# The second feed-forward product: six of its seven block products again split into seven products of halves

## The chip, the cores and the metric

The kernel runs on one core of a Trainium2 chip. Such a core has a matrix engine (TensorE, PE in the profile, with its weight loads listed apart as PEld), three engines for elementwise work (VectorE = DVE, ScalarE = ACT, GpSimd = POOL), and a queue engine (SyncE = SP) that issues the transfers between the chip's memory (HBM, "DRAM" in the code), and the on-chip memory (SBUF). Matrix products are summed in PSUM. The metric is the time of one execution in microseconds of device time (us). Lower is better.

## The reference

One layer of an encoder on a sequence of 2048 tokens, width 1024, float32: a stick-breaking attention, and behind it a feed-forward part of width 2816, each between two normalisations with a gate. This case is about the feed-forward part, and there about its last product:

```python
def swiglu_ffn(h, w_in, w_out):
    g, u = jnp.split(h @ w_in, 2, axis=-1)
    return (jax.nn.silu(g) * u) @ w_out
...
x = x + gt_f * rms_norm(y, norm_g[i, 3])
```

The first product is 2048 x 1024 times 1024 x 5632, the second (its left operand is `silu(g) * u`, "the activations" below) 2048 x 2816 times 2816 x 1024.

## The kernel before, in words

**Three products for one.** Each float32 operand is split into a high part (a copy rounded to the matrix engine's float32r, by ACT) and a low part (the operand minus the high part, by DVE or GpSimd). `mm3` (L146) then gives three matmuls, high x high (L148), high x low (L149) and low x high (L150), into the same PSUM bank. Every operand that meets the matrix engine so costs one copy and one subtraction of its size. The kernel's clock is the *slice*: one `mm3`. After each slice `tick()` (L805) runs what `after(slices, ...)` (L799) has put off until then, and moves on every generator in the list `beside` by one step. The instructions of PE, ACT, DVE and GpSimd stand in the order in which this code emits them; the transfers on SP are put in order by a scheduler of the framework. Every engine works through its own list strictly in order, and SP too: a transfer that has to wait for an engine's result or for a free buffer holds up all transfers behind it.

**The first product** (lines s in the profile) takes the tokens as two pairs of 512 (s = 0, 1) and the hidden width as 22 chunks f of 128. For each of the 44 groups (s, f) a 2 x 2 block product is made of seven block products in place of eight (Strassen-Winograd), each of four slices: 28 slices a group. For the next group, DVE makes four sums of the weights (`left_add`, L1196), and ACT and DVE split seven blocks (`left_split`, L1213, L1214). What leaves PSUM is kept by ACT (`keep`, L1296: products 1, 5 and 6, in tiles p) or added by DVE (L1348 to L1364). GpSimd multiplies gate and up of one half (tile `one`, L1360), and four more of its additions per two groups (`act_sum`, L1314) make the block sums that the second product needs; all blocks are stored to DRAM (`put_act`, L1300). Products 5 and 6 are kept in tiles of the tag "w", of which there are three: the copy of product 6 of a group needs the buffer that the `one` of the group before sets free, and product 7, two products later, is accumulated in the bank that this copy reads.

**The second product** (lines o) is one more such block product: tokens in pairs of 512, the 22 chunks of the hidden width as 11 pairs (even and odd chunk, `GO` = 11), the 1024 columns as two halves. `OUT_PRODUCTS = [1, 2, 5, 6, 4, 7, 3]` are made one after another, each in eight steps (s, i) of 11 slices: 128 tokens, 512 columns. For a step, `a_load` and `a_split` (L1238 to L1245) bring and split the left operand, ACT and GpSimd; the right operand of a product, 11 tiles of 512 columns, is loaded (`b_load`), summed by DVE (`chain_make`, L1275) and split by ACT and DVE (`b_split`, L1281, L1282) while the product before it runs. `take` (L1449, L1455) adds the bank to one or two of the four running blocks (`totals`). The last two products end output rows: square sums, norm, gate, residual (`end_square` to `end_store`), and the store.

Of the kernel before, what the change touches and what calls it, by code (L numbers as in the profile page):

```python
# [16 lines left out]
P = 128  # L17
# [10 lines left out]
EPS = 1e-6  # L28
QK_SCALE = HD ** -0.5
# [53 lines left out]
def hybrid_trunk_kernel(  # L83
# [47 lines left out]
    act_s = {  # L131
        (product, s): dram.tile([P, 4, FC // 2, P], F32, name=f"act_s{product}_{s}")
        for product in range(1, 8) for s in range(NB // 2)
    }
# [1041 lines left out]
    groups = [(s, f if s == 0 else FC - 1 - f) for s in range(NB // 2) for f in range(FC)]  # L1176
# [46 lines left out]
    GO = FC // 2  # L1223
    OUT_PRODUCTS = [1, 2, 5, 6, 4, 7, 3]
    out_steps = [(at, s, i) for at in range(7) for s in range(NB // 2) for i in range(4)]
    NSTEP = len(out_steps) // 7
    GQ = 8

    left_out, right_out, chain, out_raw, totals, totals_at = {}, {}, {}, {}, {}, {}

    def a_load(m):
        at, s, i = out_steps[m]
        src = act_s[OUT_PRODUCTS[at], s][:, i]
        parts = [
            att.tile([P, 2, n, P], F32R, name=f"ol{m}_{t}", tag=t, bufs=BUFS[t])
            for t, n in (("qt", GQ), ("aT", GO - GQ))
        ]
        nc.sync.dma_start(f32(parts[0][:, 1]), src[:, :GQ])  # L1238
        nc.sync.dma_start(f32(parts[1][:, 1]), src[:, GQ:])
        left_out[m] = parts  # L1240

    def a_split(m):
        for hl in left_out[m]:
            nc.scalar.copy(hl[:, 0], f32(hl[:, 1]))
            nc.gpsimd.tensor_tensor(hl[:, 1], f32(hl[:, 1]), f32(hl[:, 0]), op=ALU.subtract)  # L1245
# [5 lines left out]
    def b_load(at, g, which):  # L1251
        par, half = block(which)
        raw = att.tile([P, BT], F32, name=f"br{at}_{g}", tag="a", bufs=BUFS["a"])
        nc.sync.dma_start(raw, wout[half, g, :, par])
        out_raw[at, g] = raw

    def chain_tile(version, g):

        if g < 8 and g % 2 == 0:
            tag = ("wraw", "qkn")[g // 2 % 2]  # L1260
            t = att.tile([P, 2, BT], F32, name=f"ch{version}_{g}", tag=tag, bufs=BUFS[tag])
            chain[g], chain[g + 1] = t[:, 0], t[:, 1]
        elif g >= 8:
            chain[g] = att.tile([P, BT], F32, name=f"ch{version}_{g}", tag="tmp", bufs=BUFS["tmp"])

    def chain_load(version, g, which):
        chain_tile(version, g)
        par, half = block(which)
        nc.sync.dma_start(chain[g], wout[half, g, :, par])

    def chain_make(at, g):

        raw = out_raw.pop((at, g))
        a, b = (raw, chain[g]) if OUT_PRODUCTS[at] in (6, 4) else (chain[g], raw)
        nc.vector.tensor_tensor(chain[g], a, b, op=ALU.subtract)  # L1275

    def b_split(at, g):
        src = out_raw.pop((at, g)) if OUT_PRODUCTS[at] in (1, 2) else chain[g]
        tag = "kt" if (at * GO + g) % 14 < 7 else "v"
        hl = att.tile([P, 2, BT], F32R, name=f"b{at}_{g}", tag=tag, bufs=BUFS[tag])  # L1280
        nc.scalar.copy(hl[:, 0], src)  # L1281
        nc.vector.tensor_tensor(hl[:, 1], src, f32(hl[:, 0]), op=ALU.subtract)  # L1282
        right_out[at, g] = hl
# [15 lines left out]
    def put_act(product, s, f, src):  # L1299
        nc.sync.dma_start(act_s[product, s][:, :, f // 2], src.rearrange("p (i t) -> p i t", i=4))  # L1300
# [85 lines left out]
    B_FIRST = {3: 0, 4: 1, 5: 2, 7: 7, 8: 8, 9: 9, 12: 3, 14: 4, 16: 5, 18: 6, 20: 10}  # L1386
    for n, (s, f) in enumerate(groups):
# [3 lines left out]
        for at, product in enumerate(PRODUCTS):  # L1391
            acc = banks_of[{1: 0, 6: 0, 7: 0, 4: 0, 5: 1, 3: 1, 2: 2}[product]]
            for k in range(H4):
# [19 lines left out]
                if s == 0 and 4 <= f < 4 + 2 * H4:  # L1413
                    kt, second = divmod(f - 4, 2)
                    if t == 5 and not second:
                        sums_load(1, kt)
                    if t in (15, 19):
                        sums_make(1, kt, 2 * second + (t == 19))
                    if t == 25 and second:
                        sums_store(1, kt)  # L1420

                if n in (FC - 1, FC):
                    at_next = t + 4 * len(PRODUCTS) * (n - FC + 1)
                    for m in range(14):
                        if at_next == 3 + 12 * m // 5:
                            right_load(1, m)
                        if at_next == 9 + 12 * m // 5:
                            right_split(1, m)
                if n + 1 == len(groups):
                    if t in B_FIRST:  # L1430
                        b_load(0, B_FIRST[t], "ec")
                    if t - 5 in B_FIRST:
                        b_split(0, B_FIRST[t - 5])
                    if t in (9, 13, 15):
                        a_load((9, 13, 15).index(t))
                    if t in (20, 24):
                        a_split((20, 24).index(t))
            after(1, taken, n, product, banks_of)

    x1_half, end_ssq, end_rstd = {}, {}, {}  # L1440

    def take(m, acc):

        at, s, i = out_steps[m]
        product = OUT_PRODUCTS[at]
        if product == 1:
            tag = "ht" if 4 * s + i < 5 else "whl"
            totals[s, i] = att.tile([P, 4, BT], F32, name=f"tot{s}_{i}", tag=tag, bufs=BUFS[tag])
            nc.scalar.copy(totals[s, i][:, 0], acc)  # L1449
            return  # L1450
        t = totals[s, i]
        for to, add in {
            2: [(1, 0)], 5: [(2, 0)], 6: [(0, 0), (2, 2)], 4: [(0, 0)], 7: [(0, 0), (3, 2)], 3: [(2, 2)],
        }[product]:
            nc.vector.tensor_tensor(t[:, to], acc, t[:, add], op=ALU.add)  # L1455
# [4 lines left out]
    def end_square(s, i, j, half):  # L1460
        junk = att.tile([P, BT], F32, name=f"ej{s}_{i}_{j}_{half}", tag="a", bufs=BUFS["a"])
        ssq = att.tile([P, 1], F32, name=f"es{s}_{i}_{j}_{half}", tag="rms_ssq", bufs=10)
        src = totals[s, i][:, ROW[j][half]]
# [14 lines left out]
    def end_store(s, i, j):  # L1478
        rstd = end_rstd.pop((s, i, j))
        r0 = (2 * s + j) * BT + i * P  # L1480
        for half, sl in enumerate(HALVES):
            t = x1_half.pop((s, i, j, half))
            y = totals[s, i][:, ROW[j][half]]
            nc.vector.scalar_tensor_tensor(t, y, rstd, t, op0=ALU.mult, op1=ALU.add)
            nc.sync.dma_start(out[r0 : r0 + P, sl], t)

    OUT_RAW = {1: "ec", 2: "oc"}
    SUM_OF = {5: ("ed", "ec"), 6: (None, "od"), 4: (None, "oc"), 7: ("od", "ed"), 3: ("od", None)}  # L1490

    def b_events(at):

        nxt = at + 1
        if nxt == 7:
            return
        product = OUT_PRODUCTS[nxt]
        if product in OUT_RAW:
            for g in range(GO):
                if g < 3:  # L1500
                    yield 5, 2 * g, (b_load, nxt, g, OUT_RAW[product])
                else:
                    yield 6, g - 2, (b_load, nxt, g, OUT_RAW[product])
        else:
            base, other = SUM_OF[product]
            for g in range(GO):
                step, at_slice = 2 + g // 3, 3 * (g % 3) + 1
                if base:
                    yield step, at_slice, (chain_load, nxt, g, base)
                if other:  # L1510
                    yield step, at_slice, (b_load, nxt, g, other)
                    yield step + 1, at_slice, (chain_make, nxt, g)
        for g in range(GO):
            if g < 3:
                yield 6, 3 * g + 1, (b_split, nxt, g)
# [76 lines left out]
```

## Time and profile before

| | us |
|---|---|
| median of 3 runs | 2873.65 (2872.4 to 2874.76) |
| the profiled execution | 2873.52 |
| its span on the core | 2871.1 |
| first feed-forward product, 1580 to 2442 us | 862 |
| second feed-forward product, 2442 to 2861 us | 419 |
| end behind the last matmul | some 10 |
| granted TensorE clock | 0.999 of full |

The profile is one execution, taken by the hardware profiler. A line such as "L148 PE MATMUL s<-r,l 128*128 128x512 f32 x1232 | 484.5, 393 | 7.0" is a group of instructions: source line, engine, operation, output<-inputs by the names of the tiles, the shape, how often; then the time in which at least one of them ran, the mean of one in ns, and the idle time of the engine just before them with what ended it. A matmul's record is its whole passage through the array, in which the next one has already begun: two in a row overlap, so a matmul's record is longer than the distance from one start to the next. A line of the waits reads: who waited, for whom, us in total, how often, the longest. A row of the stretches has the length of the stretch and then each engine's busy time and number of instructions, the clock, the mean busy share of the 16 DMA engines, and GB/s.

### The profile page before, as it was taken

What the parts mean: (1) busy time and instruction counts of PE and PEld (TensorE: products, weight loads), DVE (VectorE), ACT (ScalarE), POOL (GpSimd) and SP (SyncE); (2) the same over time, 40 slices, a digit from 0 to 9 for tenths busy, and PEclk for the clock granted to TensorE, in tenths of its full rate; (3) what the DMA queues carried; (4) which work ended last, traced back from release to release, by engine and by line L of the source; (5) the groups of instructions that cost most, each with busy time, mean ns of one, the idle gap of its engine ahead of it and who ended that gap; (6) DMA issues with size and microseconds to landing.
All of it is one profiled execution on the core that took longest, in us unless ns stands there. A gap on an engine that the chain in (4) does not pass through costs nothing.

```text
span 2871.1 us, 41790 instructions
## 1 busy us (share of the span) xinstructions
PE 2818.2 (98%) x13848; PEld 2335.4 (81%) x13848; DVE 2027.7 (71%) x2821; ACT 1634.5 (57%) x3265; POOL 1280.4 (45%) x2032
## 2 busy tenths in 40 slices
PE   7999999999999999999999999999999999999998
PEld 6788888888888888887888788888778888888887
DVE  6788888888888888888866666555776655134377
ACT  5787777787777877778645533334433333322243
POOL 1465666576576655666410122221222222544454
PEclk9999999999999999999999999999999999999999
DMA  8765546656665635546389544334453335545575
GB/s 324 270 210 165 187 156 223 209 174 227 191 210 184 216 113 175 191 133 227 97 292 313 193 136 151 121 92 163 130 165 118 111 93 175 190 132 153 181 226 186
DMA packets 239367, 516.84 MB, mean 180 GB/s; under 512 B 22320, under 2 KB 110384, under 8 KB 221488
## 3 DMA queue, kind: packets, MB, share of 16 engines
q1 hardware_dynamic: 239152, 514.18, 55.2%
q8 instruction: 109, 1.79, 0.3%
q14 instruction: 106, 0.87, 0.1%
HBM read 346.85 MB, written 118.49 MB: 162 GB/s over the span
## 4 chain that ended last, share of the span: by engine, by line
PE 88%; DVE 5%; DMA 3%; ACT 2%; issue 1%; POOL 0%; SPq 0%; DVEq 0%; POOLq 0%; ACTq 0%
PE s L148 9%; PE s L149 9%; PE s L150 9%; PE o L586 8%; PE z L507 8%; PE t L558 8%; PE pj L148 6%; PE pj L149 6%; PE pj L150 6%; PE o L149 5%; PE o L148 5%; PE o L150 4%; PE y L148 1%; PE y L150 1%; PE y L149 1%
## 5 line engine op out<-in xcount | busy, mean ns | idle before, releaser
L548 POOL TENSOR_TENSOR a<-a,w 128x512 f32<-128x512 f32 (+3 forms) x640 | 620.5, 969 | 221.7 <-DVE w L541 131.7
L541 DVE TENSOR_TENSOR_SCAN w<-z,c,begin 128x512 f32<-128x512 f32 x384 | 489.8, 1279 | 87.1 <-ACT z L526 68.3
L148 PE MATMUL s<-r,l 128*128 128x512 f32 x1232 | 484.5, 393 | 7.0 <-DVE p L1352 4.5
L149 PE MATMUL s<-r,l 128*128 128x512 f32 x1232 | 482.0, 391 | 0.0
L150 PE MATMUL s<-r,l 128*128 128x512 f32 x1232 | 481.8, 391 | 0.0
L524 ACT ACTIVATE a<-z 128x512 f32<-128x512 f32 (+3 forms) x640 | 347.5, 543 | 171.8 <-PE z L507 140.8
L586 PE MATMUL o<-aT,v 128*128 128x512 f32 (+3 forms) x1280 | 387.5, 384 | 0.1
L574 DVE TENSOR_TENSOR aT<-t,aT 128x512 fp32r<-128x512 f32 (+3 forms) x640 | 359.4, 595 | 23.7 <-ACT aT L568 23.2
L507 PE MATMUL z<-kt,qt 128*128 128x512 f32 (+3 forms) x1280 | 363.5, 365 | 0.0
L568 ACT CAST aT<-t 128x512 fp32r<-128x512 f32 (+3 forms) x640 | 314.2, 534 | 75.7 <-PE t L558 65.5
L526 ACT ACTIVATE z<-z 128x512 f32<-128x512 f32 (+3 forms) x640 | 345.1, 539 | 0.0
L1360 POOL TENSOR_TENSOR one<-p,p 128x512 f32<-128x512 f32 x44 | 71.1, 1616 | 595.3 <-issue 307.6
L148 PE MATMUL pj<-ht,w 128*128 128x512 f32 x768 | 312.7, 407 | 7.6 <-ACT ht L693 2.6
L149 PE MATMUL pj<-ht,w 128*128 128x512 f32 x768 | 305.3, 398 | 1.2 <-DVE ht L698 0.7
L558 PEld LDWEIGHTS t<-begin,a 128*128 128x128 f32 x2176 | 255.7, 141 | 58.5 <-DVE aT L574 10.3
L150 PE MATMUL pj<-ht,w 128*128 128x512 f32 x768 | 302.8, 394 | 0.0
L558 PE MATMUL t<-begin,a 128*128 128x128 f32 x2176 | 294.7, 273 | 7.9 <-DVE aT L574 6.8
L148 PEld LDWEIGHTS s<-r,l 128*128 128x128 f32 x1232 | 231.5, 188 | 60.2 <-DVE p L1352 6.3
L150 PEld LDWEIGHTS s<-r,l 128*128 128x128 f32 x1232 | 231.5, 188 | 50.8
L149 PEld LDWEIGHTS s<-r,l 128*128 128x128 f32 x1232 | 231.6, 188 | 50.2 <-issue 0.5
L507 PEld LDWEIGHTS z<-kt,qt 128*128 128x128 f32 x1280 | 230.5, 188 | 40.1
L536 DVE TENSOR_TENSOR_SCAN w<-z,begin 128x128 f32<-128x128 f32 (+3 forms) x256 | 208.7, 818 | 76.4 <-ACT z L526 66.6
(159 smaller groups left out, 4868.1 us busy)
## 6 DMA issues: line engine op xcount, KB each, us to landing
ht<-h_s SPq DMA_DIRECT2D x108, 1024.0 KB, 8.2
wi<-in_win SPq DMA_DIRECT2D x86, 512.0 KB, 4.1
qt<-qn SPq DMA_DIRECT2D x124, 256.0 KB, 4.7
ol_qt<-act_s SPq DMA_DIRECT2D x56, 512.0 KB, 3.7
act_s<-S SPq DMA_DIRECT2D x66, 256.0 KB, 4.2
br<-in_wout SPq DMA_DIRECT2D x66, 256.0 KB, 3.5
h_s<-ht SPq DMA_DIRECT2D x16, 1024.0 KB, 7.8
o_s<-os SPq DMA_DIRECT2D x128, 128.0 KB, 2.4
```

Of the source, the lines that this page charges most:

```text
L148: nc.tensor.matmul(acc, lhs[0], rhs[0], start=first, stop=False, **kw)
L149: nc.tensor.matmul(acc, lhs[0], rhs[1], start=False, stop=False, **kw)
L150: nc.tensor.matmul(acc, lhs[1], rhs[0], start=False, stop=last, **kw)
L507: nc.tensor.matmul(z[:, :n], q[:, e, part, r * P : (r + 1) * P], k[:, e, :n], start=part == 0, stop=part == 1,)
L524: nc.scalar.activation(a[:, :n], z[:, :n], AF.Sigmoid, scale=QK_SCALE)
L526: nc.scalar.activation(z[:, :n], z[:, :n], AF.Sigmoid, scale=-QK_SCALE)
L541: nc.vector.tensor_tensor_scan(rest[:, rev], left[:, rev], begin[:, :BT][:, rev], initial=carries[r], op0=ALU.mult, op1=ALU.bypass,)
L548: nc.gpsimd.tensor_tensor(a[:, :n], a[:, :n], rest[:, 1 : n + 1], op=ALU.mult)
L558: nc.tensor.transpose(pt[:, rb * P : (rb + 1) * P], weighed[i, rb][:, j * P : (j + 1) * P], ident)
L568: nc.scalar.copy(hl[:, 0, t0:], pt[:, t0:])
L574: nc.vector.tensor_tensor(hl[:, 1, t0:], pt[:, t0:], f32(hl[:, 0, t0:]), op=ALU.subtract)
L586: nc.tensor.matmul(acc[:, t0:], lhs, hl[:, part, t0:], start=sc == qb and j == 0 and part == 0, stop=sc == 0 and j == 3 and part == 1,)
```

## The change

Products 1, 2, 5, 6, 4 and 7 (`TWICE`) of the second product are themselves made of seven products of halves: 10 of the 11 pairs of chunks are taken as 5 + 5 (`J2` = 5), the 512 rows of a token block and the 512 columns as 256 + 256 (`HT`). The eleventh pair is added as a remainder, product by product. Product 3 stays as it was.

- A step v is now (product, one of `SUBS` = [1, 2, 6, 5, 7, 3, 4], s): two row blocks of 128 times five slices, with 256 columns each, and behind four of the seven subproducts (`REST`) two slices for the remainder. There are 84 steps, 84 x 10 + 48 x 2 = 936 slices, then product 3 with 88.
- Each step splits its own left operand, 1280 columns in three pieces (`sub_left_split`; the subtraction by GpSimd for s = 0 and by DVE for s = 1), each pair of steps a right operand of the same size (`sub_right_split`, DVE), each product a remainder (`rem_split`). Loads stand four steps ahead of their use, splits two.
- Banks are added and taken apart by `sub_taken`: kept (ACT), added (DVE, `sub_add`), and put to the running blocks (`sub_total`, GpSimd for three of the four blocks, DVE for the fourth).
- The operands' sums are formed during the first product and parked in DRAM. A generator `sum_stream` in `beside` starts at group 1, a second one at group 6. Each unit takes 12 slices: its loads, 8 slices later (`SUM_LEAD`) four GpSimd additions, one a slice, then its stores. There are 11 units of weight sums (loads 2 x 512 KB, additions of 512 columns, stores 4 x 256 KB), 30 of right halves and 60 of left halves (load 512 KB, additions of 256 columns, store 512 KB). The first stream makes the 11, then the 30, then joins the second in the 60, which wait until the activations that they need are put. By count of slices the 11 are emitted in groups 1 to 5, the 30 and 20 of the 60 in groups 6 to 18.
- Weight blocks that need no sum are copied from DRAM to DRAM (33 copies of 256 KB). As they wait for nothing, the scheduler has put them early in SP's list, among the transfers of the kernel's start.
- All these units use the four buffers of the tag "aT". In SP's list the loads of a unit mostly stand behind the stores of the unit before it, and these wait for its GpSimd additions.
- The chunks run in the order 20, 21, 0 to 19, and back for s = 1. `b_load` to `b_events` are gone; `act_s` is now per s for product 3, and the blocks of the others go to `raw_s` and `rem_s`.

```diff
+    order = list(range(2 * J2 * 2, FC)) + list(range(2 * J2 * 2))
+    groups = [(0, f) for f in order] + [(1, f) for f in order[::-1]]
...
+    def half_split(hl, eng):
+        nc.scalar.copy(hl[:, 0], f32(hl[:, 1]))
+        eng.tensor_tensor(hl[:, 1], f32(hl[:, 1]), f32(hl[:, 0]), op=ALU.subtract)
...
+    def sub_left_split(v):
+        for hl in left_out[v]:
+            half_split(hl, nc.vector if v % 2 else nc.gpsimd)
...
+    def combine(steps):
+        for to, a, b, op in steps:
+            nc.gpsimd.tensor_tensor(to, a, b, op=op)
+            yield
+
+    def weight_sums(g):
+        c, d = [att.tile([P, 2, BT], F32, name=f"ws{g}_{h}", tag="aT", bufs=BUFS["aT"]) for h in range(2)]
+        nc.sync.dma_start(c, wout[0, g])
+        nc.sync.dma_start(d, wout[1, g])
+        for product, half, par in ((1, 0, 0), (2, 0, 1), (3, 1, 1)):
+            nc.sync.dma_start(b1_s[product][:, g], wout[half, g, :, par])
+        for _ in range(SUM_LEAD):
+            yield
+        yield from combine([
+            (c[:, 0], d[:, 0], c[:, 0], ALU.subtract), (d[:, 0], d[:, 1], d[:, 0], ALU.subtract),
+            (d[:, 1], d[:, 1], c[:, 0], ALU.subtract), (c[:, 1], c[:, 1], d[:, 1], ALU.subtract),
+        ])
+        for product, t in ((5, c[:, 0]), (7, d[:, 0]), (6, d[:, 1]), (4, c[:, 1])):
+            nc.sync.dma_start(b1_s[product][:, g], t)
...
+    def left_sums(product, s, j):
+        while put.get((product, s, j), 0) < 2:
+            yield
+        t = att.tile([P, 2, 2, 2 * P], F32, name=f"as{product}_{s}_{j}", tag="aT", bufs=BUFS["aT"])
+        nc.sync.dma_start(t, raw_s[product, s][:, :, :, j])
+        for _ in range(SUM_LEAD):
+            yield
...
+        nc.sync.dma_start(sum_s[product, s][:, :, :, j], t)
...
+                if n == 1 and t == 0:
+                    beside.append(sum_stream(
+                        [weight_sums(g) for g in range(GO)]
+                        + [right_sums(p, j) for p in TWICE for j in range(J2)]
+                    ))
+                if n == 6 and t == 0:
+                    beside.append(sum_stream([]))
...
+    def sub_total(eng, product, s, src, row, col):
+        for to, add in DEST[product]:
+            eng.tensor_tensor(
+                total_block(s, row, to, col), src, total_block(s, row, add, col), op=ALU.add
+            )
...
-    for m, (at, s, i) in enumerate(out_steps):
+    for v, (at, u, s) in enumerate(sub_steps):
...
+        for i in range(2):
+            rows = slice(i * HT, (i + 1) * HT)
+            for j in range(J2):
+                r = right_out[n][j // 2]
+                mm3(main[:, rows], sub_left(v, j, i), (r[:, 0, j % 2], r[:, 1, j % 2]),
+                    sub in (1, 2, 5) and i == j == 0, j == J2 - 1, skip_group_check=True)
+                tick()
+                if slot == 0 and v + 4 < len(sub_steps):
+                    sub_left_load(v + 4)
+                if slot == 1 and v + 2 < len(sub_steps):
+                    sub_left_split(v + 2)
```

395 lines of the change are left out of this document (271 added, 124 removed).

## The prediction

> **What bounds the kernel now.** I read the page's head and the busy time by stretches first, then the waits of PE, and only then the groups of the two stretches that the change touches.
>
> ```profile
> span 2871.1 us, 41790 instructions
> PE 2818.2 (98%) x13848; PEld 2335.4 (81%) x13848; DVE 2027.7 (71%) x2821; ACT 1634.5 (57%) x3265; POOL 1280.4 (45%) x2032
> ...
> PE 88%; DVE 5%; DMA 3%; ACT 2%; issue 1%; POOL 0%; SPq 0%; DVEq 0%; POOLq 0%; ACTq 0%
> ```
> ```profile
> core 0: us, PE busy (x) PEld busy (x) DVE busy (x) ACT busy (x) POOL busy (x), PEclk, DMA share, GB/s
> 0.00:25.00 25.00, 11.27 (x43) 9.97 (x44) 13.24 (x27) 15.49 (x21) 4.36 (x11) 1.00 0.93 355
> 75.00:100.00 25.00, 23.68 (x124) 19.15 (x123) 16.68 (x31) 16.10 (x32) 5.29 (x12) 1.00 1.02 344
> 1600.00:1950.00 350.00, 348.02 (x1537) 285.60 (x1537) 208.51 (x297) 130.04 (x231) 82.62 (x56) 1.00 0.43 133
> 1580.00:2442.00 862.00, 853.00 (x3732) 697.34 (x3731) 535.03 (x744) 326.08 (x584) 203.62 (x134) 1.00 0.44 137
> 2442.00:2861.00 419.00, 418.62 (x1842) 345.52 (x1841) 190.99 (x265) 143.66 (x248) 213.82 (x131) 1.00 0.58 180
> ```
> ```profile
> PE o L150 <- POOL ol_qt L1245: 0.4, 1, 0.4
> ```
>
> PE is the bound nearly throughout: 853 of 862 us in the first feed-forward product, 418.6 of 419 in the second, where its only wait is the last row, 0.4 us. So a matmul saved in the second product is time saved, as long as the operands keep coming; and what the change adds to the first product is free only in so far as it stays off PE. GpSimd is idle for 658 us there, the DMA engines for more than half.
>
> **The change, part by part.**
>
> *Matmuls of the second product.* They fall from 616 slices of 512 columns to 88 of those and 936 of 256. What a matmul of 256 columns takes from start to start is seen where the attention has two in a row, each with its own weights:
>
> ```profile
> L507 PE MATMUL z<-kt,qt 128*128 128x512 f32 x896 | 282.5, 396 | 0.0
> ...
> L507 PE MATMUL z<-kt,qt 128*128 128x256 f32 x128 | 25.3, 279 | 0.0
> ```
> ```profile
> 476.84 0.39 PE L507 MATMUL z<-kt,qt 128*128 128x256 f32 x2
> 477.07 0.39 PE L148 MATMUL pj<-ht,w 128*128 128x512 f32 x1
> ```
>
> A pair is busy for 25.3/64 = 395 ns, of which the second's passage is 279: start to start 116 ns, against 282.5/448 - 396 = 235 at 512. The timeline says the same (two in 0.23 us). In the second product a 512 takes 418.62/1842 = 227 ns. I take 116 for 256: 2808 x 0.116 + 264 x 0.227 = 325.7 + 60 = 386 against 418.6, **-33 us**. Ends: half of 227 would give -40, 120 ns -22.
>
> *Load of the engines in the second product.* Two of its 84 steps take PE 66.9 matmuls, 7.8 us. The price of a subtraction when GpSimd and DVE work at once is the point here:
>
> ```profile
> 1778.00 1.29 POOL L1314 TENSOR_TENSOR S<-one,one 128x512 f32<-128x512 f32 x1
> 1779.37 1.30 POOL L1314 TENSOR_TENSOR one<-p,one 128x512 f32<-128x512 f32 x1
> 1780.63 1.74 POOL L1314 TENSOR_TENSOR S<-S,p 128x512 f32<-128x512 f32 x1
> 1782.45 1.62 POOL L1314 TENSOR_TENSOR S<-p,S 128x512 f32<-128x512 f32 x1
> ```
> ```profile
> 1779.72 1.49 DVE L1214 TENSOR_TENSOR l<-wi,l 128x512 fp32r<-128x512 f32 x1 [1.21 <-ACT l L1213]
> 1781.14 0.68 DVE L1364 TENSOR_TENSOR p<-s,p 128x512 f32<-128x512 f32 x1
> 1781.74 1.18 DVE L1196 TENSOR_TENSOR ls<-wi 128x512 f32<-128x512 f32 x1
> 1782.84 1.78 DVE L1214 TENSOR_TENSOR l<-wi,l 128x512 fp32r<-128x512 f32 x1
> ```
>
> A DVE operation with one operand from PSUM (L1364) takes 0.68 beside GpSimd; those with both from SBUF take 1.18 to 1.78. The first starts 0.35 into a GpSimd addition and ends 0.54 behind its end, and GpSimd's next addition takes 1.74 instead of 1.29: the two wait for each other, some 0.45 us a time. Two steps hold six such operations of DVE, and of GpSimd three splits (2 x 1.29 + 0.74), 1.2 additions of 512 to the running blocks (1.55) and a share of the remainder (0.4): 5.2 + 6 x 0.45 = 7.9 us of GpSimd against PE's 7.8. There is no reserve; ends 0 (splits are two steps ahead) and 30 us, taken **+10**, near the low end, because the balance is nearly even. (0.74 for 256 columns: on the line through 1.29 at 512 and 2.40 at 1024, the median of the next row.)
>
> ```profile
> L1245 POOL TENSOR_TENSOR ol_qt<-ol_qt x56: 2392/2403/4722, 2438.7 to 2849.8; 128x1024 fp32r<-128x1024 f32 x56
> ```
>
> ```profile
> L1281 ACT CAST b<-ch 128x512 fp32r<-128x512 f32 x55 | 32.6, 620 | 21.2 <-PE o L150 19.6
> ```
>
> ACT copies three operands of 1280 columns in two steps, at 620 ns for 512 that is 4.7 us in 7.8; DVE's own work is 4.7 as well. Both are hidden by PE, as long as a late GpSimd does not hold them. Loads are 1.97 MB per two steps, 254 GB/s, under the 344 to 355 of the opening rows.
>
> *Operand sums beside the first product: work.* A group is 862/44 = 19.6 us, a slice 0.70. In groups 6 to 18, GpSimd gets 15 to 16 additions of 256 columns (11.5 us) beside its own `one` (1.6) and half of four sums (2 x 1.45): 16 us; DVE's eleven two-operand subtractions a group add 11 x 0.45 = 5: 21 us in 19.6. In groups 1 to 5 it is 9 additions of 512, 13 us instead of 11.5. The DMA: 11 + 30 + 20 units move 23 + 31.5 + 21 MB in the first 18 groups, 216 GB/s on top of 133: 349, as much as the busiest rows ever show (344 at a share of 1.02).
>
> *The same: order.* What counts is the chain of a unit. A 512 KB load lands in about 4 us, and SP waits for engines in order:
>
> ```profile
> wi<-in_win SPq DMA_DIRECT2D x86, 512.0 KB, 4.1
> ...
> act_s<-S SPq DMA_DIRECT2D x66, 256.0 KB, 4.2
> ```
> ```profile
> SPq L1300 <- POOL one L1360: 173.8, 21, 14.8
> ```
>
> In SP's list the next unit's loads stand behind this unit's stores, which wait for its last addition. Weight sums: two loads land in 4.1 + 512 KB at 350 GB/s (1.5) = 5.6 us, four additions at a mean of 1.45 take 5.8, one issue 0.3: 11.7 us for what is emitted every 12 slices, 8.4 us. Each of ten units falls 3.3 us behind, 33 in all. That reaches PE through GpSimd's order: `one` of a group stands behind the unit, and the copy of product 6 waits for `one`:
>
> ```profile
> 1757.07 1.61 POOL L1360 TENSOR_TENSOR one<-p,p 128x512 f32<-128x512 f32 x1 [11.45 <-DVE p L1352]
> ```
> ```profile
> 1769.63 0.59 ACT L1296 COPY p<-s 128x512 f32<-128x512 f32 x1 [1.67 <-PE s L150]
> ```
>
> `one` ends at 1758.7, the next group's third copy starts at 1769.6, and PE needs the bank one product (2.75 us) after that: 13 us of grace. Lost: 33 - 13, and 7 for a third of the activations' own 22 us that I count as not hidden in the load waits: 27. Then 20 pairs of a right and a left unit: strictly in turn 5.6 + 8 x 0.74 + 0.7 = 12.2 against 8.4, 76 us in all; with the next load passing before the second's additions, 9.0, 12 us. SP's list has some of each: 30. Together **+57 us** on the first product. Ends: 12, if the loads always land in the 8 slices given (then only 21 - 19.6 over 18 groups, 25, less the 13), and 110 (27 + 76, and landings later than 4.1 on a full queue). I stay in the middle: the byte count leaves the queue no slack, but a PE that has been slowed gives time back.
>
> *Copies of 33 x 256 KB at the start.* They meet a share of 0.8 to 1.0: 8.65 MB at 350 GB/s is 25 us of transfers, between 85 and 165 us, in stretches where PE has about 1 us in 25 idle; loads for the attention stand behind them. 0 to 10, taken **+3**.
>
> *At nothing:* the order of the chunks (same work) and the end behind the last matmul (same chain of square sum, norm, gate and store).
>
> Sum, from the profiled 2873.5, which stands 0.1 us from the median: 2873.5 - 33 + 10 + 57 + 3 = **2910 us**, 1.3% slower. No change is what lies within 0.2% (6 us), about what a measurement of this kernel can tell.
>
> **The rivals.**
>
> *The sums ride along (faster).* GpSimd's 658 idle us speak for it, and that its additions can run ahead of their slices. Then the first product loses at most its 12: 2873.5 - 33 + 10 + 3 = 2853, 2841 to 2865 by the ends. It decides at `one`: it must not come more than 13 us late. Against it: the 11.7 against 8.4, whose every term is a row. If a unit's chain were 9.5, the loss would be gone. Chance 0.24; gain and loss cancelling within 6 us, 0.03.
>
> *The second product becomes bound by GpSimd and DVE.* With PE no longer the longest (7.9 against 7.8) and each late split holding up the next load, it loses 40 to 60 instead of 10: 2940 to 2960. Against it: splits two steps ahead. 0.12.
>
> *Half the columns don't take half the time (the change doesn't do what it says).* A weight load's record is 188 ns (345.52/1841 in the table of stretches); were it the pace, 2808 x 0.188 + 60 = 588, +169 in place of -33: about 3110. The Trainium skill goes further ("TensorE: Matmul & The Clock Gate", Part 3, "The mechanism"): there a weight load overlaps running matmuls only when the row group differs, which all-row loads never do; with its 107 ns for 128 columns and 109 for a stream of 256 that would be an estimated 216 x 2808 = 606. This case's trace disagrees: PE and PEld are busy 418.62 and 345.52 us of the same 419. 0.03.
>
> **How the numbers follow.** Forecast 0.58, 2875 to 2960 by its own ends; the faster rival 0.24; cancelling 0.03; second product bound 0.12; columns 0.03. The range 2842 to 2970 leaves out the last and the edges. Faster 0.24, same 0.03, slower 0.73.
>
> **What would show it.** Matmuls of the second product at 112 to 120 ns start to start, its stretch 380 to 420 us. In the first product a stretch of its first 18 groups of over 390 us instead of 350, and PE's or ACT's waits naming GpSimd's `one` (L1504 now) or, behind it, the copy of product 6; SP waiting for the additions of line 1367; a DMA share near 0.9. I am wrong if those groups take 350 us (loads landed in time, and the port between DVE and GpSimd costs less than 0.45 a meeting), or if the second product's PE waits for splits.

## The result, and the profile after

The changed kernel takes 3058.18 us (median of four runs, 3054.44 to 3060.58) against 2873.63 of the kernel before: a ratio of 1.064, with a 95% interval of 1.062 to 1.066. The prediction had 2910, range 2842 to 2970: the sign was right, the size not. First the head of the page of the changed kernel, with its busy times and its chain by engine:

```profile
span 3057.9 us, 46221 instructions
PE 2851.5 (93%) x15072; PEld 2406.8 (79%) x15072; DVE 2291.2 (75%) x2975; ACT 1725.0 (56%) x3529; POOL 1741.9 (57%) x2520
...
PE 22%; DMA 8%; POOL 6%; DVE 5%; issue 2%; SPq 1%; ACT 1%; DVEq 0%; POOLq 0%; ACTq 0%
```

PE's busy time grew by only 33 us while the span grew by 187. The shares of the chain don't compare with those of before as they stand: here it is followed back only to 1692 us, 45% of the span (99% before), and PE has 22 of these 45, where it had 88 of 99. Then the stretches that the prediction's table had: the first product, the six products of halves, the last block product, the end.

```profile
core 0: us, PE busy (x) PEld busy (x) DVE busy (x) ACT busy (x) POOL busy (x), PEclk, DMA share, GB/s
1581.40:2599.00 1017.60, 894.04 (x3732) 722.51 (x3731) 595.26 (x740) 323.91 (x581) 575.95 (x537) 0.94 0.69 225
2599.00:2954.80 355.80, 341.31 (x2809) 336.33 (x2808) 318.60 (x319) 206.32 (x439) 264.69 (x185) 0.99 0.81 262
2954.80:3044.60 89.80, 68.27 (x267) 53.55 (x265) 74.00 (x101) 29.71 (x72) 39.74 (x31) 0.87 0.58 196
3044.60:3057.90 13.30, 0.34 (x2) 0.00 (x0) 7.15 (x15) 2.06 (x6) 1.10 (x2) 0.69 0.44 158
```

The first product, where nothing of PE's work was changed, takes 1017.6 us in place of 862: 155 of the 185 us. The six products of halves take 355.8, six sevenths of the 419 before would be 359: next to nothing is saved. The last block product, unchanged, takes 89.8, the pause at its beginning included, where a seventh was 60, and the end behind the last matmul 13.3 where it was 8.4.

The waits of the first product, and from SyncE's own waits over the whole span the stores of the left halves' sums:

```profile
POOL as L1367 <- DMA as<-raw: 199.6, 44, 13.1
ACT p L1432 <- POOL one L1504: 79.1, 13, 9.5
PE s L162 <- DVE p L1496: 78.3, 9, 16.5
DVE ts L1147 <- DMA ts<-h_s: 45.0, 3, 17.4
PE s L162 <- ACT p L1432: 39.4, 15, 6.1
```
```profile
SPq L1410 <- POOL as L1367: 159.8, 57, 6.8
```

The forecast's signs are there: `one` (L1504) holds up ScalarE, SyncE waits for the additions of L1367, and the first 18 groups take 474 us (355 before; over 390 was the sign). But the larger wait of PE is another one: VectorE's addition of product 7 (L1496) nine times, up to 16.5 us. One such pause, in group 10, in SyncE's list, then VectorE's, then PE's:

```profile
1864.94 1.15 SPq L1198 DMA_DIRECT2D wi<-in_win  x2
1869.06 0.57 SPq L1403 DMA_DIRECT2D as<-raw  x1
1869.67 0.63 SPq L1443 DMA_DIRECT2D raw<-one  x1
1870.35 1.29 SPq L1138 DMA_DIRECT2D ts<-h_s  x2
1871.74 0.60 SPq L1395 DMA_DIRECT2D b_s<-rs  x1
1878.71 0.56 SPq L1410 DMA_DIRECT2D sum<-as  x1
```
```profile
1878.18 1.05 DVE L1147 TENSOR_TENSOR ts<-ts 128x512 f32<-128x512 f32 x1 [13.88 <-DMA ts<-h_s]
...
1882.78 0.68 DVE L1496 TENSOR_TENSOR p<-s,p 128x512 f32<-128x512 f32 x1
```
```profile
1883.51 0.80 PE L162 MATMUL s<-r,l 128*128 128x512 f32 x1 [12.89 <-DVE p L1496]
1884.10 0.63 PE L163 MATMUL s<-r,l 128*128 128x512 f32 x1
1884.53 0.63 PE L164 MATMUL s<-r,l 128*128 128x512 f32 x1
...
1889.22 0.40 PE L163 MATMUL s<-r,l 128*128 128x512 f32 x1
1889.46 0.40 PE L164 MATMUL s<-r,l 128*128 128x512 f32 x1
1889.70 0.40 PE L162 MATMUL s<-r,l 128*128 128x512 f32 x1
```

Tiles ts are VectorE's sums of the second pair of token blocks (`sums_load`, `sums_make`, groups 4 to 11, in the kernel before as well). Their load goes out at 1870.35, behind transfers of the streams; it lands at 1878; VectorE has stood still for 13.88 us by then, with the addition that PE needs behind it in its list. PE gets it at 1883.5, and then runs its matmuls 0.43 us apart for another 5.3 us, before they return to 0.23: the granted clock was at half. Over the first product the clock stood at half for 130 us, but mostly while PE waited anyway; counted over the matmuls' starts, 154 came at 0.38 to 0.48 us, a cost of 30 us. The distances of over 0.5 us between starts hold 138 us above the even pace, against 15 before: 123 us more of pauses proper. These two make up 153 of the 155. The Trainium skill has the rule ("TensorE: Matmul & The Clock Gate", Part 1, "HAM oscillation — how this bites in real kernels"): waits for transfers that are longer than its activity window (about 3.4 us there) drop the clock to half, and each is paid again at the restart. This trace agrees in the main: of its 17 stretches at half clock 14 go with the 14 pauses of over 3.4 us between two starts; the other three come behind pauses of 2.5 to 2.9 us.

### The profile page after: what moved, and what is told of

The parts are those of the page before. It is cut to its first block, busy times and chain, and to the rows that moved or that the text cites. A ratio compares the mean times of both kernels' runs of the same rounds, so it can differ in the third digit from the quotient of the medians.

```text
span 3057.9 us, 46221 instructions
## 1 busy us (share of the span) xinstructions
PE 2851.5 (93%) x15072; PEld 2406.8 (79%) x15072; DVE 2291.2 (75%) x2975; ACT 1725.0 (56%) x3529; POOL 1741.9 (57%) x2520
## 5 line engine op out<-in xcount | busy, mean ns | idle before, releaser
L162 PE MATMUL s<-r,l 128*128 128x512 f32 x1232 | 502.5, 408 | 118.0 <-DVE p L1496 78.3
L163 PE MATMUL s<-r,l 128*128 128x512 f32 x1232 | 496.4, 403 | 0.0
L164 PE MATMUL s<-r,l 128*128 128x512 f32 x1232 | 494.8, 402 | 0.0
L162 PEld LDWEIGHTS s<-r,l 128*128 128x128 f32 x1232 | 240.4, 195 | 182.0 <-DVE p L1496 83.4
L1367 POOL TENSOR_TENSOR as<-as 128x256 f32<-128x256 f32 x240 | 214.2, 893 | 250.3 <-DMA as<-raw 199.6
L1230 DVE TENSOR_TENSOR l<-ls,l 128x512 fp32r<-128x512 f32 x172 | 160.9, 936 | 188.0 <-ACT l L1229 187.6
L164 PEld LDWEIGHTS s<-r,l 128*128 128x128 f32 x1232 | 240.1, 195 | 53.9
L163 PEld LDWEIGHTS s<-r,l 128*128 128x128 f32 x1232 | 240.7, 195 | 52.0 <-issue 0.5
```

The lines of the kernel that those rows point to most:

```text
L162: nc.tensor.matmul(acc, lhs[0], rhs[0], start=first, stop=False, **kw)
L163: nc.tensor.matmul(acc, lhs[0], rhs[1], start=False, stop=False, **kw)
L164: nc.tensor.matmul(acc, lhs[1], rhs[0], start=False, stop=last, **kw)
L1367: nc.gpsimd.tensor_tensor(to, a, b, op=op)
```

## The experiments

"First product" is the time from its first matmul to its last one in each run's profile: 862.3 us before, 1017.7 in the change. Where no interval is given, a time is that of one run. A first theory was the queue theory: late ts loads are the cause. The recorded one is called the order theory; the other theories are explained in the expectations.

**1. No sums at all.**

```diff
-        6: (sum_s, 0, 0), 3: (sum_s, 0, 1), 7: (sum_s, 1, 0), 5: (sum_s, 1, 1),
+        6: (raw_s, 0, 0), 3: (raw_s, 0, 1), 7: (raw_s, 1, 0), 5: (raw_s, 1, 1),
...
-                        + [right_sums(p, j) for p in TWICE for j in range(J2)]
...
-                    beside.append(sum_stream([]))
```

> Leaves out the sums of halves: both sum streams keep only the copies of weight blocks, and the second product reads raw blocks wherever it would read sums (so its numbers aren't those of the reference; its instructions, shapes and bytes are). It divides the 185 us that the change costs between the two products. All theories on the first product (below) expect it back at 860 to 870 us (1018 with the sums, 862 before the change), so 2900 to 2905 us in all, if the second product stays at 445 us. If the second product is dearer for reasons that lie in the first one (clock, late stores, a backlog), it falls below 435 us; if GpSimd and VectorE hold it up by themselves, it stays at 440 to 450 us.

The first product took 862.9 us, as expected, the rest 454.2 (458.9 in the change, 429.1 before): the first product's loss is all the streams', and of the 30 us that the rest loses 25 are there without them.

**2. No token sums.** `sums_load(1, ...)`, `sums_make`, `sums_store` in groups 4 to 11 left out.

> Leaves out the VectorE sums of the second pair of token blocks (tiles ts), their loads and their stores in groups 4 to 11; products 4 to 7 of that pair then read raw blocks. The sum streams stay as they are. Queue theory (the loads of these tiles stand behind the streams' stores in SyncE's order and take turns in the same four buffers, VectorE waits for them in its order, and everything behind it waits too): the four pauses in groups 4, 6, 8 and 10 go, the first product falls from 1018 us by 60 to 100 us. Order theory, the recorded one (the multiplication to one stands behind a unit's additions in GpSimd's order): the groups 1 to 11 stay long, the first product falls by 20 us at most.

989.8 us, 28 less, between the two forecasts and nearer to the order theory's 20: groups 4, 6, 8 and 10 fell from 35 to 43 us to 20 to 26, but the groups between and behind them rose, up to 34 us in group 5 (19.2 before). PE's wait for ScalarE's copies, the recorded route, rose from 39.4 to 68.3 us. So late ts loads are not the one cause: without them most of the time shows elsewhere.

**3 and 4. Transfers alone, additions alone.**

```diff
 def combine(steps):
     for to, a, b, op in steps:
-        nc.gpsimd.tensor_tensor(to, a, b, op=op)      # run 3: left out; run 4: kept, on one still tile, without loads and stores
         yield
```

> Leaves out the streams' additions on GpSimd: the same tiles are loaded and stored in the same order, the stored sums are the raw blocks. Order theory and port theory (GpSimd beside VectorE): the first product returns to 862 to 880 us. Transfer theory (the streams' 250 GB/s slow every other transfer): it stays above 980 us. Queue theory: the stores no longer wait for GpSimd, so the queue only waits for loads; 870 to 920 us.

> Leaves out the streams' loads and stores: the same additions with the same shapes are made at the same places in the order, on one tile that lies still; the second product reads raw blocks. Order theory: one still falls behind the additions where they crowd, the first product at 900 to 920 us (57 us of sums as forecast, or less where additions no longer wait for loads). Port theory: the same, but spread over all groups with VectorE's instructions lengthened. Queue theory: nothing is held up in SyncE's order, the pauses in groups 4, 6, 8 and 10 go, the first product at 862 to 885 us.

915.5 and 877.9 us: 53 and 15 us more than before. Both lie where the queue theory had them (870 to 920, 862 to 885) and outside the order theory's ranges; 34 of the 53 us of run 3 stand in groups 4, 6, 8 and 10, those with ts loads. Together transfers and additions cost 155, so 87 us are there only when both are. The same stretch, 1622 to 1900 us, of four kernels, columns as above: before, transfers alone, additions alone, the change.

```profile
1622.00:1900.00 278.00, 278.00 (x1220) 228.25 (x1219) 166.41 (x233) 99.17 (x176) 71.52 (x47) 1.00 0.45 139
```
```profile
1622.00:1900.00 278.00, 251.02 (x1069) 204.33 (x1069) 147.19 (x207) 87.78 (x155) 62.41 (x41) 0.94 0.92 308
```
```profile
1622.00:1900.00 278.00, 274.38 (x1193) 223.89 (x1192) 210.35 (x227) 97.84 (x173) 244.92 (x235) 0.99 0.43 136
```
```profile
1622.00:1900.00 278.00, 212.91 (x870) 171.33 (x869) 148.16 (x167) 73.24 (x129) 172.23 (x155) 0.87 0.77 257
```

At this pace the transfers alone fill 0.92 of the DMA engines, and the additions alone 245 of 278 us of GpSimd. In the change each falls back (0.77 and 172), and PE with them: 213 us. The waits shown with the result say that GpSimd and the loads wait for each other. The fall is also one of pace: the change gets through 870 of 1220 matmuls here (0.71), and the sums are emitted by slices, so GpSimd's 172 are 0.70 of its 245. A look at the change alone shows two engines with a quarter and more to spare.

**5 to 7. Stores later, streams later.** If SyncE's wait for the additions is the link between the two, a store put into its list later breaks it (5); if ts, a start behind it (6); 7 has both.

```diff
-    SUM_LEAD = 8
+    SUM_LEAD, STORE_LAG = 8, 6      # run 5; in run 7: 3
...
+        for _ in range(STORE_LAG):
+            yield
         nc.sync.dma_start(sum_s[product, s][:, :, :, j], t)      # likewise the other two
...
-                if n == 1 and t == 0:      # first stream; second: n == 6
+                if n == 12 and t == 0:      # both, runs 6 and 7
```

> Everything is computed; each unit's stores are put into SyncE's order six slices (some 4 us) later. Interlock theory (GpSimd's additions wait for loads that stand in SyncE's order behind a store of the other stream, and that store waits for GpSimd): SyncE no longer waits for additions, the 87 us that transfers and additions cost only together go, and what is left is 53 us of transfers and 15 us of additions: the first product at 900 to 950 us (1018 before), 2950 to 2985 us in all. Transfer theory (the loads are late because the memory traffic of 250 GB/s is): no change, above 1000 us.

> Everything is computed; both streams start at group 12, behind the last sums of the token blocks (tiles ts). Interlock theory: the pauses of the ts loads go (53 us in the run with transfers alone), the interlock goes on from group 12 to the end of the streams: the first product at 945 to 985 us. Queue theory (it is the ts loads that are held up, VectorE and everything behind it wait): 862 to 900 us. Order theory of the prediction: not below 920 us.

> Everything is computed; both streams start at group 12, and each unit's stores come three slices later. Interlock theory: neither the ts loads nor SyncE's waits for additions are left, the first product at 870 to 895 us (862 before the change, and 15 us for the additions as measured alone), 2905 to 2935 us in all. Transfer theory: above 930 us.

986.4, 1068.0 and 1027.9 us. Run 5 wins 31 us, less than half of what it should; 6 and 7 are worse than the change itself, where 945 to 985 and 870 to 895 were expected. By group 12 the activations of the next units lie ready, so little holds the streams back, and the same work is pressed into fewer groups: eleven of the groups 14 to 28 took over 30 us each in run 6.

On the interlock these runs don't decide, because the lag didn't do what was expected of it. SyncE's waits for the additions in the first product, the change first, then run 5:

```profile
SPq L1410 <- POOL as L1367: 159.8, 57, 6.8
SPq L1395 <- POOL rs L1367: 81.7, 26, 6.1
SPq L1384 <- POOL ws L1367: 67.2, 44, 4.4
```
```profile
SPq L1416 <- POOL as L1367: 115.8, 42, 4.4
...
SPq L1399 <- POOL rs L1367: 57.1, 22, 4.0
SPq L1386 <- POOL ws L1367: 55.4, 32, 5.6
```

228 us of 309 are left. And as the lag is part of a unit, a unit comes every 18 slices in run 5 and every 15 in run 7, where the change has 12: run 5 is a thinner stream too, and what of its 31 us is the lag's is not known.

**9. `one` on VectorE.**

```diff
-            nc.gpsimd.tensor_tensor(one, gate1, up1, op=ALU.mult)
+            nc.vector.tensor_tensor(one, gate1, up1, op=ALU.mult)
```

> Everything is computed; only the multiplication to one, which stands behind the streams' additions in GpSimd's order, is made by VectorE. Order theory, the recorded route (GpSimd late, so one late, so the copy of product 6 that needs its buffer late, so the matmuls late): the waits of ScalarE's copies for one go, and the first product falls from 1018 us to 915 to 965 us; what is left are the pauses of the ts loads in groups 4 to 10. If the path is another (the token sums, left operands or right operands arriving late): above 990 us.

1019.0 us: nothing. The route of the prediction is cut (no wait of ScalarE for `one` is left), and its time turns up elsewhere, in waits of the run's first product:

```profile
PE s L162 <- DVE p L1496: 99.1, 10, 25.3
...
DVE ls L1212 <- DMA wi<-in_win: 61.5, 9, 15.2
...
PE s L162 <- ACT p L1432: 34.2, 9, 9.9
```

The weights of the next groups (tiles wi) are now what comes late. So the recorded route was real but, in the change, not what set the end.

**10. The sums on VectorE.** `nc.vector` for `nc.gpsimd` in `combine`.

> Everything is computed; the streams' additions are made by VectorE in place of GpSimd, at the same places. Port theory (GpSimd's additions and VectorE's instructions lengthen each other): the low halves of the left operands return from 950 to 750 ns and the first product falls below 940 us. Late-load theory (whatever engine makes the sums in its order stands still when a load isn't there, and the loads aren't): VectorE's additions that the matmuls wait for stand behind the sums, and the first product stays above 1000 us.

993.4 us. The port is really freed (the low halves of the left operands' sums: 951 ns in the change, 709 here, over 1900 to 2200 us), and yet 24 of 155 us is all that it brings. Neither forecast of the time was met (below 940, above 1000).

**11, 13, 15. Lead, density and token sums.** In run 11 the lead is 16 slices, so a unit comes every 20 slices and no longer every 12. Run 13 is run 11 without the token sums. Run 15 has the density of run 11 with the old lead.

```diff
-    SUM_LEAD = 8
+    SUM_LEAD = 16                      # runs 11 and 13, until group 38
...
+        for _ in range(8):             # run 15: behind a unit's stores, until group 38
+            yield
```

> Everything is computed; a unit's load is put into SyncE's order 16 slices (11 us) ahead of its additions in place of 8 (5.5 us; a load takes 4.8 to 5.0 us from issue to landing), until group 38; the streams so run longer and thinner. Late-load theory: GpSimd's waits for as, rs and ws loads fall from 212 us to under 60 us, and the first product falls to 900 to 950 us (ts pauses and 15 us of additions are left). Buffer theory (four buffers, of which the ts tiles hold two: a longer hold makes SyncE wait for buffers): above 1000 us.

> Leaves out the VectorE sums of the second pair of token blocks (ts) as in the second run, and has the lead of 16 slices. Late-load theory (954 us with the long lead, of which 45 us are pauses in groups 6 and 8): 905 to 920 us in the first product, clean groups from 4 to 20. Buffer theory or another cause: above 935 us, the lost time turning up in other groups as it did when the token sums alone were left out (990 us).

> Everything is computed; the lead stays at 8 slices, and each stream rests 8 slices behind a unit's stores, so that a unit comes every 20 slices as with the long lead (12 in the change). Late-load theory: the loads are as late as in the change, the first product stays at 990 us or above (954 with the long lead). Density theory (transfers at 0.91 to 0.94 of the DMA engines and GpSimd at 0.86 to 0.94, each measured alone at the change's density, cannot both be kept up through one queue and four buffers): as good as the long lead or better, 925 to 965 us.

954.0, 913.3 and 972.9 us. Run 11 is 4 us above what the late-load theory expected. In it, groups 10 to 20 are at 19.2 us again (19.5 in group 10). GpSimd's waits for its loads fell from 264 to 114 us, not under 60, and the token sums' pause is still there:

```profile
POOL as L1367 <- DMA as<-raw: 80.7, 23, 12.2
...
DVE ts L1147 <- DMA ts<-h_s: 41.5, 2, 30.3
```

Run 15 says which half of it counts more: of the 64 us that run 11 wins, 45 come with the thinner streams alone and 19 with the earlier load. 973 lies between the two forecasts, nearer to that of the density. SyncE waits as long for the additions in run 15 as in the change (311 and 309 us), so the length of that wait is not what sets the time. Run 13 was forecast within its range: with thin streams the token sums' share can be taken away (41 us), which in the dense ones of run 2 mostly moved. Its remaining 51 us stand in group 1 (5.5), group 9 (4), groups 21 and 22, where the second pair's right operands are loaded (11), and groups 26 to 28, where the late modulation loads weights into the same four buffers (30).

**14. Three overlaps moved away** (token sums, early streams, late modulation), all sums made.

```diff
-                if 4 <= n < 4 + 2 * H4:      # token sums: four tiles in eight groups
+                if 2 <= n < 2 + H4:          # one tile a group
...
-                if n == 1 and t == 0:        # first stream; lead 14
+                if n == 6 and t == 0:
...
+            while group in range(25, 29):    # start no unit here
+                yield
```

> Everything is computed. The token sums come in groups 2 to 5, one tile a group, the streams start at group 6 with a lead of 14 slices, start no unit in groups 25 to 28 (the late modulation's weight loads), and the second product's low halves are VectorE's. Late-load theory: the first product at 875 to 895 us (862 before the change; 15 us of additions), the second at 434 us and the end as now: 2895 to 2925 us, 1 to 2% slower than before the change. If a cause is missing: above 910 us in the first product. No theory has it faster than before: the six products of halves take 343 us at best here, the last product and the end 100.

2977.5 us, 1.036 of the kernel before (1.034 to 1.038); the first product 950.8, not 875 to 895. That is above the 910 that the expectation gave for a cause still missing. Each overlap taken away did vanish: groups 2 to 8 at 19.2 to 19.3 us, groups 26 to 28 at the 19.2, 20.1 and 20.9 of the kernel before. But 88 us are lost all the same, 43 in groups 9 to 17 and 32 in groups 21 and 22, where the second pair's right operands are still loaded. Nearly all of PE's waits are here those of the recorded route, for the copies that wait for `one`:

```profile
PE s L162 <- ACT p L1438: 64.8, 15, 19.1
ACT p L1438 <- POOL one L1510: 60.6, 11, 10.9
...
PE s L162 <- DVE p L1502: 6.7, 3, 4.9
```

Density alone doesn't explain this run. Run 5 has a unit every 18 slices as well; in groups 14 to 18, where both runs make right and left sums, it lost 1 us and run 14 lost 16. From 1871 to 1967 us run 5 kept 0.83 of the DMA engines and 82 of 96 us of GpSimd busy, with PE busy for 95.5. The two differ in the lag of the stores, the lead, and in that run 14 starts both streams at once, so that their additions come by turns in the same slices (as in runs 6 and 7, which were the worst). In runs 11 and 15 they come by turns too, at 20 slices, and cost 0 and 3 us in groups 11 to 18. Which of these counts was not separated.

**8. The second product's low halves on VectorE.**

```diff
-            half_split(hl, nc.vector if v % 2 else nc.gpsimd)
+            half_split(hl, nc.vector)
...
-        half_split(left_rem[at][:, s], nc.gpsimd)
+        half_split(left_rem[at][:, s], nc.vector)
```

> Everything is computed; in the second product the low halves that GpSimd makes (left operands of the even steps, left remainders) are made by VectorE; GpSimd keeps the totals of three of the four blocks, and the last block product is as it was. Port theory (VectorE and GpSimd lengthen each other's instructions: the low half of a right operand takes 1427 ns beside GpSimd and 685 ns alone): VectorE's mean for that row falls below 1000 ns, its busy time a product stays at or below 50 us of 58, the six products fall from 356 us to 338 to 350 us. If the two engines don't hold each other up, VectorE gets 10 us more of work a product, becomes the bound, and the six products rise above 358 us.

The six products took 343.4 us in place of 355.8, as the port theory said. The groups of low halves between 2600 and 2943 us, first of the change, then of this run:

```profile
L1262 POOL TENSOR_TENSOR sl<-sl 128x512 fp32r<-128x512 f32 x82 | 119.8, 1481 | 42.4 <-ACT sl L1261 33.3 <-DMA sf<-sum 6.4 <-DMA ol_qt<-act_s 2.7
L1262 DVE TENSOR_TENSOR sr<-sr 128x512 fp32r<-128x512 f32 x82 | 113.9, 1427 | 32.0 <-ACT sr L1261 32.0
...
L1262 DVE TENSOR_TENSOR sl<-sl 128x512 fp32r<-128x512 f32 x80 | 85.4, 1107 | 3.2 <-ACT sl L1261 3.2
```
```profile
L1262 DVE TENSOR_TENSOR sl<-sl 128x512 fp32r<-128x512 f32 x166 | 142.2, 896 | 37.7 <-ACT sl L1261 37.7
...
L1262 DVE TENSOR_TENSOR sr<-sr 128x512 fp32r<-128x512 f32 x82 | 53.7, 694 | 0.0
```

A right operand's low half takes 694 ns where it took 1427. VectorE makes twice the left halves, and the remainders, and is busy for less: 296 us in these 343, 307 in the change's 344. What GpSimd did here was paid for in full by VectorE's waiting. The Trainium skill says as much ("SBUF — State Buffer", "Who interferes with whom"): an instruction of VectorE with two inputs in SBUF and one of GpSimd that reads there contend, and whichever is first has the shared pair of ports for its whole length. The 1427 ns against 694 agree.

**12 and 16. The last block product.** Both are run 8 with one more edit.

```diff
-        acc = bank("y", m % 4, f"o{m}")
+        acc = bank("y", (m + 2) % 4, f"o{m}")                # run 12
...
-                after(6 + 10 * i, x1_reload, s, i, 1)        # run 16: in the last product's second half
-                end_whole(s, i, 1, 16 + 10 * i)
```

> Everything is computed; the run with splits on VectorE, and the last block product begins with the PSUM buffers of tags acc and z in place of t, which the last sums of the six products still hold. If the pause of 8.8 us at that change is the matmuls waiting for VectorE to empty the last sums: it falls below 3 us, and the second product from 445 us (span 3046) by 5 to 8 us. If it is the low half of the left operand (GpSimd) or the right operands' loads: no change.

> Everything is computed; beside the splits on VectorE, the output rows that were finished while the last halves product ran (four blocks: reload of x1, squares, norm, stores) are finished during the last block product, in its second half. If the pauses of 8.8 and 6.9 us at the beginning of the last product come from that work, which stands ahead of the right operand's loads in SyncE's order and ahead of its low halves in VectorE's: both fall below 3 us, and second product and end together from 467 us to 450 to 458 us. If the right operand's loads wait for buffers that the last halves product holds: the second pause stays.

Run 12: 446.7 us from the last matmul of the first product to the end, 446.5 in run 8; the pause moved behind the first matmuls. (The 467 us in the second text should read 447; what it expects is a fall of 9 to 17.) In run 16 the two pauses of 8.8 and 6.9 us went. The waits at that change, run 8 first:

```profile
ACT b L1261 <- DMA b<-b_s: 12.4, 1, 12.4
...
PE o L162 <- DVE tot L1625: 8.5, 1, 8.5
...
PE o L163 <- DVE b L1262: 6.4, 1, 6.4
```
```profile
ACT b L1261 <- DMA b<-b_s: 5.5, 1, 5.5
...
PE o L162 <- DVE tot L1625: 1.1, 1, 1.1
...
PE o L163 <- DVE b L1262: 0.3, 1, 0.3
```

So the output rows of the kernel's end, in the lists of SyncE and VectorE, held up the right operand and the emptying of the banks. The matmuls are through 9 us sooner (423.9 us behind the first product, 433.2 in run 8), but the rows that were put off come 7 us later behind them (20.1 against 13.3): 2.5 us are won, not 9 to 17. In run 16 PE also waits 11.5 us in the last product for low halves of its left operand, which GpSimd makes there.

## Why the prediction was wrong, step by step

- *Matmuls of the second product, -33.* Nearly right in itself: the matmuls of 256 columns stand 118.1 ns apart (mean of all distances below 140 ns), not 116, which makes it -27.
- *Load of the engines there, +10 (0 to 30).* The balance was seen to have no reserve, but was then priced near the low end. It was 24 us, inside the ends: the distances above 140 ns in the six products hold that much over the even pace. Sized wrongly was the meeting of the two engines, 0.45 us each; the right operand's low half alone went from 0.69 to 1.43. Run 8 shows the mechanism: there 11.5 us are left of the 24.
- *Operand sums, +57 (12 to 110).* This is the step that failed: 155. Its "work" part had both warnings: 349 GB/s, "as much as the busiest rows ever show", and 21 us of GpSimd and VectorE in a group of 19.6. They were then used as a remark on the queue's slack, while the sum was made in its "order" part from a single chain, unit by unit, with 13 us of grace and one way out to PE, over `one`. Runs 3 and 4 confirm the two loads, at 0.92 of the DMA engines and 245 of 278 us of GpSimd. A DMA share near 0.9 was named as the sign; it shows only in the transfers alone. Run 9 shows that in the change the one way over `one` didn't set the time, run 14 that it is the main way once the ts loads are moved: there are at least two ways, and cutting one leaves the other. Between the two resources stand one list of SyncE and four buffers, and whatever has a load in that list was late in turn: token sums, weights of the next group, the late modulation. By groups, 27 us were forecast for groups 1 to 5, 30 for 6 to 18 and nothing behind; measured were 30, 89 and 36. The first agrees by luck: 24 of the 30 stand in group 4, in the pause of a ts load. The strictly-in-turn bound of 76 us for 20 pairs, of which 30 were taken, was nearer. Why transfers and additions cost 87 us more together than alone is narrowed down by the runs (a thinner stream wins 45), not settled.
- *The clock* had no term: 30 us, within the 155.
- *Copies at the start, +3:* the first product began 1.7 us later (1581.4 us), but in other runs with the same copies between 1578.1 and 1583.8: nothing that can be told from zero.
- *At nothing: the order of the chunks and the end.* The chain of the end is the same, but the step from the halves to the last product was not looked at: the last product cost 30 us more, the end 5. Run 16 shows part of the reason, output work in the lists at that place; the rest stays open.
- *The rivals.* That the second product becomes bound by GpSimd and VectorE (0.12, a loss of 40 to 60 us there) looks near in its number, since the second product with its end took 30 us more than before where 23 less were forecast. But that load cost 24 us, as the forecast's own ends allowed; the rest is the last product and the end, which the rival didn't name. The other two are excluded: nothing rode along, and half the columns did take half the time.
- *The range.* The ends of the four terms add up to 2845 and 3001, not to the 2875 and 2960 said to follow from them; 3058 lies outside both.

No run here is faster than the kernel before. Without any sums in the first product (run 1) it is still 0.8% slower (2897.8 against 2873.9 us), so the second product as it stands gives nothing to pay for the sums with; run 8's 12 us would halve that, and the sums would still have to be free.

## What to carry to other kernels

When a change adds work to two idle resources in series, price the pace at which it is emitted. Here 0.92 of the DMA engines and 0.88 of GpSimd, each reached alone, were not reached together through one in-order list and four buffers, and the loss was more than the sum of what each costs alone (155 against 15 + 53); 0.83 and 0.85 were held together in run 5. Following one chain to the bound engine is not enough then: cut it, and the next thing in the list is late; so list everything that shares the queue and the buffers, and spread the work before moving its waits about: that won 45 us here. Work given to GpSimd beside VectorE's two-operand instructions in SBUF is no relief if VectorE is near its limit (here 307 of 344 us busy).

## What the runs showed of the hardware, unexpected

- A pause costs PE more than itself: behind one of 12.9 us the matmuls stood 0.43 us apart for 5.3 us, with the granted clock at half; some 30 us in all in the first product.
- The low halves of the second product cost VectorE as much in waiting for GpSimd as they would in doing them (307 us busy in 344, and 296 in 343 with all of them).
- A busy share can hide saturation: 0.77 of the DMA engines and 62% of GpSimd was what was left of 0.92 and 88%, once everything, PE included, went at 0.71 of the pace.
